# Output projection of a hybrid decoder layer: weights two tiles at a time, GpSimd's additions and low parts in pieces

## The chip, the cores and the metric

The kernel runs on one core of a Trainium2 chip. The metric is the device time of one execution in microseconds, lower is better; the time before is the median of three runs. A core has a matrix engine (TensorE, PE in the profile), a vector engine (VectorE, DVE), an activation engine (ScalarE, ACT), GpSimd (POOL) and SyncE (SP), which issues nearly all DMAs here. Each engine executes its own instructions strictly in the order in which they were put; engines wait for each other by semaphores.

## The reference

One inference step of one layer, for a prompt of 1024 positions and 8 samples of 8 new positions (N = 1088 columns in all):

```python
h = rms_norm(x, norm_mix_g)
proj = h @ w_in                       # a convolution branch and 12 attention heads
a = silu(layer_norm(depthwise_conv(a_val * sigmoid(a_gate))))
o = attend(q, k, v)                   # dilated windows, merged by their softmax denominators
x = x + concatenate([a, o]) @ w_out   # the output projection and the residual
h = rms_norm(x, norm_ffn_g)
x = x + (silu(conv3(h @ w_ffn_gate)) * (h @ w_ffn_up)) @ w_ffn_down
y = rms_norm(x, norm_final_g)
```

The change touches the fifth line: `w_out` is 1024 x 1024, `x` is 1024 features by 1088 columns, and the residual is the layer's input.

## The kernel before

Everything is kept transposed: 128 features on the partitions, positions along the row. A product in float32 is made of three matmuls on a faster 32-bit type: each operand is split into a high part (a copy that rounds, on ACT) and a low part (the difference, on DVE or GpSimd), and high·high, high·low and low·high are summed in PSUM.

The stages in order: the input projection (`project`), one pair of heads after the other; attention for the samples (`sample_attention`) and for the prompt (`prompt_heads`), which is written around the later projections; the output projection (`out_part` and, for the last part, `out_half`); the gated feed-forward part, as products of a Strassen-like scheme; the last projection and norm.

The input of the output projection is eight tiles of 128 features, `mixed[0]` to `mixed[7]`, spilled to DRAM as they are finished. It is done in three parts along the contraction, `PARTS = (3, 3, 2)` tiles. The first two parts are `out_part` with `k0 = 0` and `k0 = 3`, each over the eight output tiles m (L881). For each m, `load_w` (L155) loads 128 x 384 weights on SP's queue into a raw buffer `wr` (two buffers, tag WR), makes the high part `wh` on ACT (L163) and the low part `wl` on GpSimd (L165) (five buffers for both together, tag W), and `gemm` (L177) does three chunks of columns (384, 384, 320), or two halves of the columns up to HN = 544 where the rest is deferred. In the part with `k0 = 0` the sums are copied out of PSUM into `x2[m]` by ACT (L895) and DVE (L897). In the part with `k0 = 3` the residual `xr` is loaded (L888, three buffers, not before the last tile of the samples' cache was loaded), GpSimd adds it to `x2[m]` (L889), and DVE adds the sums (L893). The last three m of that part are kept back until the last head's weighted sums are issued (L899), as work for PE in that head's tail. The following stage takes its first weights and two tiles `eh`, `el` (L923) from the same buffers.

Attention for the prompt, per head and half of the positions: `load_head` loads queries and keys (L620, L628) and GpSimd reorders the queries (`qw`, L622); `scores` computes scores on PE (L675) into two PSUM banks `s`, and DVE takes them out with the running minimum (L679); `exchange` (L644) passes minima between classes by a small product (L653) and small DVE operations (L650, L656, L659); L704 and L705 take the minimum of two 128 x 4 tiles; ACT exponentiates (L716); PE transposes (L743) and takes the weighted sum (L764); at the end of a pair `normalise` divides (L774 to L783).

What order the instructions of one engine have is decided when the program is built: a planner simulates the program with costs of its own and puts on each engine the instruction that is ready, by priority, so that the matmuls of `out_part` fill the gaps between attention's steps. `tc.issue_after` and `high_priority` in the code constrain it. Buffers are handed on by the planner's waits: a tile's buffer comes free when the last reader of its earlier content is done.

Of the kernel before, what the change touches and what calls it, by code (L numbers as in the profile page):

```python
# [18 lines left out]
F32 = mybir.dt.float32  # L19
# [5 lines left out]
P = 128  # L25
D = 1024
# [4 lines left out]
N = S + NS  # L31
# [39 lines left out]
HN = N // 2  # L71
# [15 lines left out]
def trunk_kernel(tc, xT, w_in, w_first, w_out, w_gate, w_up, w_down, par, kc, vc, sa, sf, pmask, smask,  # L87
                 yT, kT, vT, ca, cas, cf):
    nc = tc.nc
    with (  # L90
# [8 lines left out]
        def nm(s):  # L99
            cnt[0] += 1  # L100
            return f"{s}_{cnt[0]}"
# [26 lines left out]
        def keep(s, w=N):  # L128
            return tp.tile([P, GW], F32, tag="T", name=nm(s))[:, :w]
# [22 lines left out]
            tc.add_manual_dep(later, earlier.name, mybir.DependencyInfo(mybir.DependencyClass.NoSync,  # L152
                                                                        mybir.DependencyReason.DATA))

        def load_w(src, nk, lo_eng, new=None):  # L155

            w = nk * P
            raw = wp.tile([P, w], F32, tag="WR", name=nm("wr"), bufs=WR)
            weights_read[0] = nc.sync.dma_start(raw if len(src.shape) == 2 else
                                                raw.rearrange("p (m c) -> p m c", m=src.shape[1]), src).ins  # L160
            new = new or [lambda s: wp.tile([P, w], F32R, tag="W", name=nm(s))] * 2
            hi = new[0]("wh")[:, :w]
            nc.scalar.activation(hi, raw, AF.Copy)  # L163
            lo = new[1]("wl")[:, :w]
            lo_eng.tensor_sub(lo, raw, hi.bitcast(F32))  # L165
            return hi.rearrange("p (k c) -> p k c", c=P), lo.rearrange("p (k c) -> p k c", c=P)

        cached = []
# [8 lines left out]
        def gemm(w, x, nk, evac, banks=None, chunks=CHUNKS):  # L177


            whi, wlo = w  # L180
            order = [(c, k) for c in range(len(chunks)) for k in range(nk)]
            if banks:
                order = [(c, k) for k in range(nk) for c in range(len(chunks))]
            ps = {}
            for c, k in order:
                t0, n = chunks[c]
                if k == 0:
                    ps[c] = bank(*(banks[c] if banks else gbank[0]))[:, :n]
                xh, xl = x[k]
                nc.tensor.matmul(ps[c], whi[:, k, :], xh[:, t0:t0 + n], start=(k == 0), stop=False)  # L190
                nc.tensor.matmul(ps[c], whi[:, k, :], xl[:, t0:t0 + n], start=False, stop=False)  # L191
                nc.tensor.matmul(ps[c], wlo[:, k, :], xh[:, t0:t0 + n], start=False, stop=(k == nk - 1))  # L192
                if k == nk - 1:
                    evac(ps[c], t0, n)
# [180 lines left out]
        def a_branch(i):  # L375
# [18 lines left out]
            if i == 0:  # L394
                first_gemms(sg, gp, se)
            else:
                gate = load_w(w_in[2 + i], KT, nc.vector)
                val = load_w(w_in[i], KT, nc.vector)
                gemm(gate, h, KT, ev_gate)
                gemm(val, h, KT, ev_val)  # L400
# [43 lines left out]

        def project(p, pump):
            W = [load_w(w_in[4 + 6 * c + p], KT, nc.gpsimd) for c in range(3)]
            dq = dp.tile([2, P, S], F32, name=nm("dq"))
            dk = dp.tile([2, P, S], F32, name=nm("dk"))
# [417 lines left out]
        x2 = []  # L866
        first = [0]

        def spare(s, w=N):
            return zt("R", "x2", KT - TB, s, GW)[:, :w]  # L870
# [7 lines left out]
        def out_part(k0, part):  # L878

            n = len(part)  # L880
            for m in range(KT):  # L881
                w = load_w(w_out[m, :, k0 * P:(k0 + n) * P], n, nc.gpsimd)
                if k0 == 0:
                    x2.append(keep("x2") if m >= KT - TB else spare("x2"))
                if k0 == PARTS[0]:
                    r = staged("xr")
                    with tc.issue_after(cached[8 * NS1 + X2]):
                        nc.sync.dma_start(r, xT[m * P:(m + 1) * P, :])  # L888
                    nc.gpsimd.tensor_add(x2[m], x2[m], r)  # L889

                def ev(ps, t0, n, x=x2[m]):
                    if k0:
                        nc.vector.tensor_add(x[:, t0:t0 + n], ps[:, :n], x[:, t0:t0 + n])  # L893
                    elif t0 in ONACT:
                        nc.scalar.activation(x[:, t0:t0 + n], ps[:, :n], AF.Copy)  # L895
                    else:
                        nc.vector.tensor_copy(x[:, t0:t0 + n], ps[:, :n])  # L897

                with tc.issue_after(weighed[0]) if k0 and m >= KT - BEHIND else nullcontext():  # L899
                    gemm(w, part, n, ev, chunks=CHUNKS if k0 == 0 or m not in ORDER[:DEFER] else HALF)  # L900

        def staged(s):
            return zt("G", "XR", XR, s)
# [12 lines left out]
        with tc.issue_after(turned_out[0]):  # L916
            nc.scalar.activation(sp.tile([P, 1], F32, name="table"), ones, AF.Sqrt)
        out_part(*part)
        for n in PARTS[1:-1]:
            out_part(*load_part(n, staged, g_part))  # L920
# [22 lines left out]
        def slot(tag, s, dt=F32R, w=HN):  # L943
            return zt("F", tag, 8, s, HN, dt)[:, :w]
# [53 lines left out]
        k0 = first[0]  # L998
        n = PARTS[-1]
# [36 lines left out]
        for h, tag in enumerate(("b11", "t2")):  # L1036
# [4 lines left out]
            for m0 in ORDER[h * 4:h * 4 + 4:2]:  # L1041
                raw = slot("b11", "wr", F32, 2 * n * P)
                queued(raw.rearrange("p (m c) -> p m c", m=2), w_out[m0:m0 + 2, :, k0 * P:].rearrange("m p c -> p m c"))
                hi, lo = early["b21"].pop() if early["b21"] else slot("b21", "wh", w=512), slot("b21" if m0 == ORDER[0] else "t3", "wl", w=512)
                with tc.issue_after(last_high):
                    last_high = parts_of(raw, hi, lo)
                hi, lo = [t.rearrange("p (k c) -> p k c", c=P) for t in (hi, lo)]
                for j in range(2):
                    wl[m0 + j] = hi[:, j * n:j * n + n], lo[:, j * n:j * n + n]
        for i in range(n1):  # L1050
            lo, hi = slot("b21", "ml"), slot("t3", "mh")
            raw = lo.bitcast(F32)
# [12 lines left out]
        for m in ORDER[:DEFER]:  # L1065
            hi, lo = [slot("b22", t, w=n1 * P) for t in ("wh", "wl")]
# [91 lines left out]
        raw = [slot("t2", "wr", F32, half) for _ in range(4)]  # L1158
# [362 lines left out]
        w, act = [], []  # L1521
# [140 lines left out]
        for i, (t0, n) in enumerate(TAIL):  # L1662
            r = []
# [20 lines left out]
        v, r, t = [sp.tile([P, 9], F32, tag=tag, name=nm(tag), bufs=2)[:, :nt] for tag in ("rv", "rr", "rt")]  # L1684
# [118 lines left out]
```

## Time and profile before

| | us |
|---|---|
| median of 3 runs | 1326.91 |
| lowest and highest | 1324.6, 1328.79 |
| profiled execution | 1329.6 |
| span of its instructions | 1327.8 |
| mean granted PE clock | 0.993 |
| output projection's residual additions (L889) | 500.2 to 529.5 of the span |

The profile is of one execution. Its page gives busy time by engine, the chain of work that ended last and the costliest groups of instructions; the trace behind it answers for any stretch of time, line or tile. Times within it are microseconds from the span's start; L889 is line 889 of the kernel. A DMA's issue is an instruction of SP's queue (SPq); its landing is later. The granted clock is the share of its full clock that PE was given.

### The profile page before, as it was taken

The page shows a single profiled execution, that of the slowest core. Times are in us where ns is not written, and L with a number is a line of the kernel's source. Part 1 is how long each engine was busy: PE and PEld are TensorE (multiplying, and loading weights), DVE is VectorE, ACT ScalarE, POOL GpSimd, SP SyncE. Part 2 cuts the span into 40 slices and gives each one's busy share as a digit, 9 for nine tenths or more (in the row PEclk, how much of TensorE's full clock was granted, in tenths as well). Part 3 has the DMA queues.
Part 4 walks back from the last instruction along what each step waited for, and adds up shares of the span by engine and source line. Part 5 has one row for each costly group of instructions (what it writes and reads, how often), then busy time and mean ns, then how long its engine had stood idle before and what let it go on. Part 6 is the DMA issues. An engine that isn't in the chain of part 4 may idle for free.

```text
span 1327.8 us, 26026 instructions
## 1 busy us (share of the span) xinstructions
PE 1294.9 (98%) x10336; PEld 1253.1 (94%) x10336; DVE 939.2 (71%) x1788; ACT 562.6 (42%) x1132; POOL 474.2 (36%) x389
## 2 busy tenths in 40 slices
PE   9999999999998998999999999999999999999997
PEld 9999898999977788899999999999999999999997
DVE  7479879555674657579976677676776659967656
ACT  7322221547584564565633323332333345334433
POOL 0121112111101016141656546565564544444611
PEclk9999999999999998999999999999999999999998
DMA  9248777564789996271023331232313395352403
GB/s 309 73 152 295 263 261 192 175 170 133 221 265 286 264 298 206 67 255 43 33 91 123 107 108 63 93 123 91 122 42 114 104 342 206 108 178 96 157 32 104
DMA packets 93658, 211.43 MB, mean 159 GB/s; under 512 B 13920, under 2 KB 42720, under 8 KB 93536
## 3 DMA queue, kind: packets, MB, share of 16 engines
q1 hardware_dynamic: 92672, 208.76, 47.9%
q8 instruction: 81, 1.33, 0.4%
q10 hardware_dynamic: 864, 1.01, 0.2%
q14 instruction: 41, 0.34, 0.1%
HBM read 153.69 MB, written 56.04 MB: 158 GB/s over the span
## 4 chain that ended last, share of the span: by engine, by line
PE 78%; DVE 11%; DMA 7%; ACT 2%; issue 1%; SPq 0%; DVEq 0%; ACTq 0%
PE g L190 6%; PE g L191 6%; PE g L192 6%; PE py L955 4%; PE py L958 4%; PE py L957 4%; PE g L955 4%; PE g L958 4%; PE g L957 4%; PE pz L955 3%; PE pz L958 3%; PE pz L957 3%; PE px L955 3%; PE px L958 3%; PE px L957 3%; PE s L675 3%
## 5 line engine op out<-in xcount | busy, mean ns | idle before, releaser
L165 POOL TENSOR_TENSOR wl<-wr,wh 128x1024 fp32r<-128x1024 f32 (+1 forms) x34 | 62.0, 1823 | 313.9 <-PE g L192 191.1
L190 PE MATMUL g<-xh,wh 128*128 128x384 f32 (+1 forms) x472 | 156.8, 332 | 0.9 <-DVE qkv L467 0.9
L192 PE MATMUL g<-xh,wl 128*128 128x384 f32 (+1 forms) x472 | 155.3, 329 | 0.0
L191 PE MATMUL g<-xl,wh 128*128 128x384 f32 (+1 forms) x472 | 155.2, 329 | 0.0
L955 PE MATMUL g<-ux,as 128*128 128x272 f32 x504 | 145.1, 288 | 0.6 <-DVE x L1595 0.6
L958 PE MATMUL g<-ux,as 128*128 128x272 f32 x504 | 145.3, 288 | 0.0
L957 PE MATMUL g<-ux,as 128*128 128x272 f32 x504 | 144.7, 287 | 0.0
L1109 POOL TENSOR_TENSOR wb<-wr,wb 128x512 fp32r<-128x512 f32 x79 | 116.3, 1484 | 50.1 <-ACT wb L1108 50.1
L1505 POOL TENSOR_TENSOR as<-ar,as 128x640 fp32r<-128x640 f32 (+1 forms) x56 | 89.1, 1602 | 104.6 <-ACT as L1504 92.1
L1108 ACT ACTIVATE wb<-wr 128x512 fp32r<-128x512 f32 x79 | 49.7, 629 | 163.2 <-DVE wr L1143 104.3
L955 PEld LDWEIGHTS g<-ux,as 128*128 128x128 f32 x504 | 95.0, 189 | 1.0 <-issue 1.0
L1109 POOL TENSOR_TENSOR wa<-wr,wa 128x512 fp32r<-128x512 f32 x40 | 62.4, 1561 | 90.9 <-ACT wa L1108 89.0
L958 PEld LDWEIGHTS g<-ux,as 128*128 128x128 f32 x504 | 94.8, 188 | 0.0
L957 PEld LDWEIGHTS g<-ux,as 128*128 128x128 f32 x504 | 94.6, 188 | 0.0
L716 ACT ACTIVATE y<-y,m 128x128 f32<-128x128 f32 (+1 forms) x192 | 88.5, 465 | 10.6 <-DVE m L704 9.3
L1373 DVE SCALAR_TENSOR_TENSOR fc<-gb,prm,fc 128x1104 f32<-128x1104 f32 x44 | 82.2, 1888 | 14.7 <-ACT fc L1371 14.4
L190 PEld LDWEIGHTS g<-xh,wh 128*128 128x128 f32 x472 | 88.7, 188 | 3.0 <-DVE qkv L467 1.5
L191 PEld LDWEIGHTS g<-xl,wh 128*128 128x128 f32 x472 | 88.8, 188 | 0.1
L192 PEld LDWEIGHTS g<-xh,wl 128*128 128x128 f32 x472 | 88.8, 188 | 0.0
L417 DVE SCALAR_TENSOR_TENSOR cacc<-gp,prm,cacc 128x1024 f32<-128x1024 f32 x60 | 84.2, 1404 | 0.1
L679 DVE CUSTOM_DVE_ANT_0 y<-s,pmk 128x128 f32<-128x128 f32 (+1 forms) x192 | 63.6, 375 | 25.5 <-PE s L675 22.7
L163 ACT ACTIVATE wh<-wr 128x1024 fp32r<-128x1024 f32 (+1 forms) x36 | 29.6, 821 | 121.0 <-PE g L192 93.4
(413 smaller groups left out, 4309.3 us busy)
## 6 DMA issues: line engine op xcount, KB each, us to landing
cr<-in_kc SPq DMA_DIRECT2D x24, 768.0 KB, 8.5
cr<-in_vc SPq DMA_DIRECT2D x24, 768.0 KB, 8.7
ux<-ub SPq DMA_DIRECT2D x63, 272.0 KB, 4.2
kk<-dk SPq DMA_DIRECT2D x48, 256.0 KB, 6.3
wr<-in_w_in SPq DMA_DIRECT2D x20, 512.0 KB, 5.2
wr<-in_w_gate SPq DMA_DIRECT2D x20, 512.0 KB, 3.3
wr<-in_w_up SPq DMA_DIRECT2D x20, 512.0 KB, 4.6
ub<-u SPq DMA_DIRECT2D x18, 544.0 KB, 4.0
```

What stands on the lines that cost most here:

```text
L190: nc.tensor.matmul(ps[c], whi[:, k, :], xh[:, t0:t0 + n], start=(k == 0), stop=False)
L191: nc.tensor.matmul(ps[c], whi[:, k, :], xl[:, t0:t0 + n], start=False, stop=False)
L192: nc.tensor.matmul(ps[c], wlo[:, k, :], xh[:, t0:t0 + n], start=False, stop=(k == nk - 1))
L417: eng.scalar_tensor_tensor(acc[:, :S], gp[:, j:j + S], col(w0 + j), acc[:, :S], op0=ALU.mult, op1=ALU.add)
L679: nc.vector.tensor_tensor_reduce(out=y[:, o:o + n], in0=ps[:, o:o + n], in1=mask, op0=ALU.add, op1=ALU.min, scale=1.0, scalar=3e38, accum_ ...
L716: nc.scalar.activation(y, y, AF.Exp, bias=m[:, 4 * g + i:4 * g + i + 1], scale=-1.0, accum_out=den[:, g, 2 * hd + u, i:i + 1])
L955: nc.tensor.matmul(ps, whi[:, k, :], xh[:, t], start=(start and k == 0), stop=False, skip_group_check=True)
L957: nc.tensor.matmul(ps, whi[:, k, :], xl[:, t], start=False, stop=False, skip_group_check=True)
L958: last = nc.tensor.matmul(ps, wlo[:, k, :], xh[:, t], start=False, stop=(stop and k == nk - 1), skip_group_check=True).ins
L1109: nc.gpsimd.tensor_sub(lo, x, hi.bitcast(F32))
L1373: nc.vector.scalar_tensor_tensor(c[:, :W], gb[i][:, t:t + W], col(C_FW + 3 * f + t), c[:, :W], op0=ALU.mult, op1=ALU.add)
L1505: nc.gpsimd.tensor_sub(lo, raw, hi.bitcast(F32))
```

## The change

`load_w` gets a parameter `cut`: the low part is made by instructions of at most `cut` columns instead of one. `out_part` calls it for every second m, with the weights of m and m + 1 in one DMA and one raw buffer (128 x 768), one high part of 768 columns on ACT, and three low parts of 256 columns on GpSimd; each m takes its half of both. The residual is added in four pieces of 272 columns. The bytes, the matmuls and the DVE instructions stay the same.

```diff
-        def load_w(src, nk, lo_eng, new=None):
+        def load_w(src, nk, lo_eng, new=None, cut=D):
...
             lo = new[1]("wl")[:, :w]
-            lo_eng.tensor_sub(lo, raw, hi.bitcast(F32))
+            for c in range(0, w, cut):
+                t = slice(c, min(c + cut, w))
+                lo_eng.tensor_sub(lo[:, t], raw[:, t], hi.bitcast(F32)[:, t])
...
             for m in range(KT):
-                w = load_w(w_out[m, :, k0 * P:(k0 + n) * P], n, nc.gpsimd)
+                if m % 2 == 0:
+                    both = load_w(w_out[m:m + 2, :, k0 * P:(k0 + n) * P].rearrange("m p c -> p m c"), 2 * n, nc.gpsimd,
+                                  cut=2 * P)
+                w = [t[:, m % 2 * n:m % 2 * n + n] for t in both]
...
-                    nc.gpsimd.tensor_add(x2[m], x2[m], r)
+                    for c in range(0, N, HN // 2):
+                        t = slice(c, c + HN // 2)
+                        nc.gpsimd.tensor_add(x2[m][:, t], x2[m][:, t], r[:, t])
```

`load_w` is also called for `w_in` in the input projection, with `cut` at its default of 1024 columns, which is one instruction as before.

## The prediction

> **What bounds the kernel now.** The page of the profile is read first: busy time by engine and the chain that ended last.
>
> ```profile
> PE 1294.9 (98%) x10336; PEld 1253.1 (94%) x10336; DVE 939.2 (71%) x1788; ACT 562.6 (42%) x1132; POOL 474.2 (36%) x389
> ...
> PE 78%; DVE 11%; DMA 7%; ACT 2%; issue 1%; SPq 0%; DVEq 0%; ACTq 0%
> ```
>
> TensorE (PE) is busy for all but 1327.8 − 1294.9 = 32.9 us of the span, so an edit that touches no matmul can win only time in which PE stands idle or runs at a lower granted clock. The second view is therefore busy time by stretches of 10 us over the output projection, which runs interleaved with the last attention heads. Columns: stretch, its length, busy us of PE, PEld, DVE, ACT and POOL with their instructions, granted clock, DMA share, GB/s.
>
> ```profile
> 500.00:510.00 10.00, 6.17 (x34) 5.85 (x33) 9.39 (x25) 4.92 (x19) 9.78 (x4) 0.71 0.86 257
> 510.00:520.00 10.00, 10.00 (x122) 9.35 (x122) 8.29 (x20) 3.45 (x11) 7.19 (x5) 0.95 0.61 154
> ```
>
> One stretch stands out: from 500 to 510 PE has 6.17 us of work, the clock falls to 0.71, and GpSimd (POOL) is busy for 9.78. The same view cut at the stall, and the waits of PE from 410 to 560 (who waited, for whom, us in total, times, longest):
>
> ```profile
> 502.30:506.06 3.76, 0.00 (x1) 0.01 (x1) 3.69 (x8) 2.98 (x13) 3.76 (x3) 0.76 0.68 218
> 506.06:511.00 4.94, 4.94 (x20) 4.94 (x21) 3.86 (x18) 0.38 (x1) 4.52 (x3) 0.50 1.03 291
> ```
>
> ```profile
> PE s L675 <- DVE st L679: 3.8, 1, 3.8
> PE o L764 <- DMA vw<-dv: 2.6, 1, 2.6
> PE ss L568 <- DMA cr<-in_kc: 2.6, 1, 2.6
> ```
>
> PE stands still for 3.76 us and then works 4.94 us at half clock. It waits for the minimum of the scores (L679, on VectorE, DVE), which frees the score banks. What held L679 is in the order of time on DVE and POOL (start, us, engine, line):
>
> ```profile
> 500.24 2.50 DVE L705 TENSOR_TENSOR m<-st,xr 128x4 f32<-128x4 f32 x1
> 502.67 0.27 DVE L659 TENSOR_REDUCE xr<-xf 128x32 f32<-128x128 f32 x1
> 502.97 2.22 DVE L774 TENSOR_TENSOR dn<-xr,den 128x16 f32<-128x16 f32 x1
> 505.23 0.42 DVE L679 CUSTOM_DVE_ANT_0 y<-s,pmk 128x256 f32<-128x256 f32 x1
> ...
> 505.57 0.42 DVE L679 CUSTOM_DVE_ANT_0 y<-s,pmk 128x256 f32<-128x256 f32 x1
> 505.92 0.08 DVE L679 DVE_READ_ACCUMULATOR2_ANT st<- 128x1 f32 x1
> ```
>
> ```profile
> 500.22 9.87 POOL L889 TENSOR_TENSOR x<-x,xr 128x1088 f32<-128x1088 f32 x4 [5.35 <-DMA xr<-in_xT]
> ```
>
> ```profile
> L705 DVE TENSOR_TENSOR m<-st,xr x24: 146/152/2503, 237.6 to 544.1; 128x4 f32<-128x4 f32 x24
> ```
>
> L705 works on 4 columns. Its median is 152 ns (the row has minimum, median, maximum); here it took 2.50 us, and ended when the first of POOL's four residual additions did (500.22 + 9.87/4 = 502.69). L774 met the second one and ended with it. So a small DVE operation on SBUF that meets a POOL addition waits for that whole instruction, here twice in a row: this, not the amount of POOL's work, makes PE's stall. Between two additions DVE does get in (L705 ended before L774 was held again). L679, which reads PSUM, took its usual 0.42 beside the third addition.
>
> **The change, part by part.** The sum is made against the profiled execution, 1329.6 us (span 1327.8 and 1.8 around it).
>
> *The residual additions in pieces.* Eight instructions of 1088 columns become 32 of 272; two of 384 columns for the low parts become three of 256. POOL has rows for nearly these sizes:
>
> ```profile
> L889 POOL TENSOR_TENSOR x<-x,xr 128x1088 f32<-128x1088 f32 x8 | 20.1, 2528 | 11.2 <-DMA xr<-in_xT 11.2
> L165 POOL TENSOR_TENSOR wl<-wr,wh 128x384 fp32r<-128x384 f32 x16 | 16.2, 1012 | 119.9 <-PE g L192 73.2 <-PE r L192 16.4 <-PE ss L558 15.0
> L1652 POOL TENSOR_TENSOR x<-x,rb 128x256 f32<-128x256 f32 x4 | 2.9, 740 | 20.9 <-ACT rb L241 20.9
> ```
>
> 256 columns cost 740 ns; the slope from 384 to 1088 columns is (2528 − 1012)/704 = 2.15 ns a column, so 272 cost 0.740 + 16 × 0.00215 = 0.775 us. Replay the stall: the first piece runs 500.22 to 501.00; L705 ends at 501.15; L659 adds 0.27 (501.42); L774 meets the second piece, which began near 501.15 and ends at 501.93, and ends at 502.11; two L679 with their accumulator reads take 505.23 to 506.00, 0.77 us, so the bank is free at 502.9. PE's previous matmul ended here:
>
> ```profile
> 501.89 0.34 PE L192 MATMUL g<-mh,wl 128*128 128x384 f32 x1
> 506.06 2.08 PE L675 MATMUL s<-kk,qw 128*128 128x256 f32 x8 [3.83 <-DVE st L679]
> ```
>
> The gap shrinks from 3.83 to 502.9 − 502.23 = 0.7 us: **−3.1 us**. Bounds: 0, if DVE is not let in between pieces; −3.83, if L705 and L774 meet none.
>
> *The half clock behind it.* 4.94 us at 0.50 are 2.47 us of work at full clock, so without the drop **−2.5 us**; bounds 0 and −2.5. Whether a gap brings a drop isn't read from its length alone:
>
> ```profile
> 410.00:413.00 3.00, 1.10 (x8) 0.81 (x6) 0.00 (x0) 0.49 (x1) 0.00 (x0) 1.00 1.02 313
> 413.00:416.40 3.40, 2.65 (x25) 2.32 (x26) 0.49 (x3) 0.00 (x0) 0.00 (x0) 1.00 1.04 416
> ...
> 547.00:549.50 2.50, 1.36 (x6) 0.90 (x8) 0.34 (x2) 2.15 (x8) 0.00 (x0) 0.83 0.91 278
> 549.50:552.50 3.00, 3.00 (x18) 2.25 (x17) 0.90 (x4) 0.05 (x1) 0.00 (x0) 0.58 0.47 160
> 552.50:555.00 2.50, 1.53 (x12) 1.06 (x10) 1.81 (x3) 1.73 (x4) 0.00 (x0) 1.00 0.00 0
> ```
>
> A gap of 2.65 us (the wait for vw) left the clock at 1.00, while 1.14 us of idle time in 2.5 us was followed by 0.58. I take the whole drop as gone, since a gap of 0.7 among busy matmuls is the smallest of these. [...]
>
> *POOL's longer work.* The additions grow from 20.1 to 32 × 0.775 = 24.8 us, the low parts from 16.2 to 24 × 0.740 = 17.8 us. POOL's idle time covers that: from 500 to 520 it is busy 9.78 + 7.19 of 20 us. What is queued behind on POOL is the reordering of a head's queries (qw, L622):
>
> ```profile
> 511.46 1.04 POOL L622 CAST qw<-qs 128x1024 fp32r<-128x1024 f32 x1
> ```
>
> ```profile
> 516.66 1.09 PE L675 MATMUL s<-kk,qs 128*128 128x128 f32 x8
> ...
> 521.34 0.83 PE L675 MATMUL s<-kk,qw 128*128 128x128 f32 x5
> ```
>
> Four additions take 16 × 0.775 = 12.4 instead of 9.87 us, and a pair's low part 2.2 instead of 1.0, so L622 would start 3.7 us later and end near 516.2. PE, 5.6 us earlier, would want it at 521.34 − 5.6 = 515.7: **+0.5 us**, or nothing if the planner puts the cast between pieces. SyncE (SP) is held by the same additions, for the three buffers of xr:
>
> ```profile
> 496.04 7.04 SPq L888 DMA_DIRECT2D xr<-in_xT  x4
> 503.17 1.09 SPq L620 DMA_DIRECT2D qs<-dq  x2
> ```
>
> and for that L620:
>
> ```profile
> DMA to landing us min/median/max: 5.0/5.4/5.9
> ```
>
> The fourth xr waits for the first addition (4 × 0.775 = 3.1 instead of 2.5 us), so the queries behind it leave 0.6 us later. They take 5.4 us to land (503.8 + 0.5 + 5.4 = 509.7 for the second) and are wanted at 516.66 − 5.6 = 511.1: nothing.
>
> *Two tiles at once.* Sixteen loads of 192 KB become eight of 384 KB, the same bytes. The five buffers of high and low parts and the two raw buffers then hold 4.5 tiles (0.88 MB) more ahead, moved in front of attention's loads in the one SP queue: at the 291 GB/s above 3.0 us, the upper end, since PE already waits for DMAs twice (2.6 and 2.6). But those early loads are issued where the queue is not full:
>
> ```profile
> 360.00:370.00 10.00, 10.00 (x75) 9.37 (x74) 4.08 (x17) 3.35 (x10) 0.00 (x0) 1.00 0.19 78
> 370.00:380.00 10.00, 9.48 (x90) 8.73 (x88) 7.64 (x40) 7.42 (x25) 2.50 (x4) 1.00 0.80 214
> ```
>
> Free shares of 0.81 and 0.20 of 10 us are 10 us of transfer, three times what is needed. I take **+0.5 us**, near the lower end. ACT's splits (16 of 384 columns become 8 of 768) get no dearer and lie off the path: nothing. The gain that deeper filling may bring lies in the tail above, 547 to 555: idle 1.14 + 0.97 and clock losses of 0.17 × 1.36 + 0.42 × 3.00 = 1.5, in all 3.6 us. I count none of it, since those gaps are waits inside the last head, not for weights.
>
> **Sum:** −3.1 − 2.5 + 0.5 + 0.5 = **−4.6 us**: 1325.0 for a profiled execution. The median before, 1326.9, lies 2.7 us under the profiled one; the same sum on it gives **1322.3 us**.
>
> **Rivals.**
>
> 1. *The clock drop was the profiled execution's own.* For it: the 2.7 us between the profile and the median are nearly the 2.5 of the drop. Against it: drops follow smaller gaps too, as shown. The gain is then 3.1 − 1.0 = 2.1: 1324.8. [...]
>
> 2. *The stall survives or moves*, the change not doing what it says: POOL's pieces follow each other so closely that DVE loses each time, or the planner, which orders every engine by its own estimates, puts other DVE operations of the path beside the adds. Against it: DVE got in between the additions above. Price: nothing gained, 1.0 paid, 1327.9.
>
> 3. *SP's queue is blocked longer: slower.* SP issues in order, and a weight load waits there until the raw buffer's low part is done, which waits for matmuls:
>
> ```profile
> SPq L159 <- POOL wl L165: 25.2, 5, 9.5
> ```
>
> The longest such wait is 9.5 us; a pair is released by two tiles instead of one, so a wait of 19 us is possible. A head's queries are used 516.66 − 503.17 = 13.5 us after their issue; from there on it costs. PE would stop 5.5 us and, as at 506, lose 2.5 more: 8.0, less the 4.6 gained, is +3.4: 1330.3. Twice, it is 1338. Against it: buffers for five tiles need fewer loads late in the stage.
>
> **How the numbers follow.** Forecast 50% (its own range 1318 to 1324.5, reaching down by the 0.7 left of the gap and the 3.6 of the tail), rival 1 15%, rival 2 17%, rival 3 18%. A measurement of this kernel tells about 0.3%, 4.0 us, from no change: faster means below 1322.9, slower above 1330.9. Faster: 0.8 of the forecast and a fifth of rival 1, 0.43. Slower: 0.15 of rival 3 and 0.02 of rival 2, 0.17. Within: 0.40. The range 1318 to 1331 leaves out the lowest of the forecast (some 5%) and most of rival 3 (some 15%).
>
> **What would show it.** In the profile after: L889 32 times near 0.78 us; L705 and L774 nowhere above about 0.95 us; PE's longest wait for L679 below 1 us; clock 1.00 where the residual additions run; POOL's busy time up by 6 us; w_out loads of 384 KB, with SP's wait for L165 no longer than 9.5 us. Wrong would make it: a PE wait of more than 3 us for qs, qw, kk or vw, or a new one for DVE elsewhere from 380 to 570; weight loads standing on the chain; or a time that moves in stages that the diff doesn't touch, where the planner has reordered work.

## The result, and the profile after

| | before | after |
|---|---|---|
| median of 5 runs each, same chip (us) | 1325.54 | 1320.51 |
| lowest and highest | 1324.6, 1328.79 | 1316.28, 1322.68 |
| profiled execution, its span | 1329.6, 1327.8 | 1317.16, 1315.4 |
| mean granted PE clock | 0.993 | 0.997 |

The ratio of the times is 0.9949, with the interval [0.9925, 0.9974]: 5.0 us faster by the medians, where 4.6 were predicted. The two profiled executions differ by 12.4 us, more than the medians do. So the change is judged by the medians, and the profiles are used for where time is lost.

The page after: busy time by engine, and the chain that ended last.

```profile
PE 1290.3 (98%) x10336; PEld 1250.4 (95%) x10336; DVE 926.6 (70%) x1788; ACT 561.1 (43%) x1124; POOL 479.9 (36%) x421
...
PE 81%; DVE 11%; DMA 5%; issue 1%; ACT 1%; SPq 0%; POOL 0%; DVEq 0%; ACTq 0%
```

PE still bounds the kernel. POOL is busy for 5.7 us more (479.9 against 474.2); the residual's pieces had been priced at 4.7 us more and the low parts' at 1.6. The stretch with the stall, by 10 us, after:

```profile
500.00:510.00 10.00, 9.86 (x129) 8.96 (x128) 8.74 (x28) 5.80 (x20) 7.50 (x10) 1.00 0.98 265
510.00:520.00 10.00, 10.00 (x74) 9.39 (x74) 5.85 (x17) 2.64 (x4) 6.98 (x11) 1.00 0.83 273
```

PE is busy for 9.86 of the first 10 us instead of 6.17, and the clock is 1.00 instead of 0.71 and 0.95. What PE waited for between 380 and 570, after (lines stand two, later seven higher than before: L679 is L681, L889 is L896):

```profile
PE o L766 <- DMA vw<-dv: 2.7, 1, 2.7
...
PE s L677 <- DVE st L681: 0.4, 1, 0.4
```

The wait of 3.83 us is down to 0.4. The wait for vw stays as it was (2.6). POOL in order of time after, and the minimum, median and maximum of the residual pieces:

```profile
514.66 8.78 POOL L896 TENSOR_TENSOR x<-x,xr 128x272 f32<-128x272 f32 x12 [3.02 <-DMA xr<-in_xT]
523.40 2.13 POOL L167 TENSOR_TENSOR wl<-wr,wh 128x256 fp32r<-128x256 f32 x3
525.48 5.86 POOL L896 TENSOR_TENSOR x<-x,xr 128x272 f32<-128x272 f32 x8
```

```profile
L896 POOL TENSOR_TENSOR x<-x,xr x32: 750/774/960, 502.5 to 530.5; 128x272 f32<-128x272 f32 x32
```

A piece takes 774 ns at the median (775 were worked out). From 514.66 to 531.34 POOL runs 23 of them without a break: such an unbroken row of POOL instructions is called a train below. Of the small DVE operations that meet this train, the one held longest, after:

```profile
520.47 0.80 DVE L707 TENSOR_TENSOR m<-st,xr 128x4 f32<-128x4 f32 x1
```

It waited for one piece. Each of these signs is as the prediction named it. Two things are not yet answered by it: whether the pieces bring the gain, or the weights in pairs do, which came with them; and whether the clock would have dropped in most runs before.

The part of the stage ahead of the residual additions gives a first hint. Busy time from 400 to 500 and from 500 to 560, before, after, and in a kernel that has the pieces alone (resid_only below), in this order:

```profile
400.00:500.00 100.00, 93.55 (x916) 81.52 (x916) 57.12 (x229) 52.89 (x153) 11.44 (x13) 1.00 0.96 284
500.00:560.00 60.00, 52.93 (x480) 48.17 (x479) 38.15 (x111) 29.42 (x91) 26.00 (x14) 0.91 0.46 136
```

```profile
400.00:500.00 100.00, 97.06 (x997) 85.48 (x995) 59.15 (x252) 57.36 (x170) 14.39 (x19) 1.00 0.95 286
500.00:560.00 60.00, 57.59 (x500) 54.27 (x499) 36.16 (x101) 29.08 (x80) 37.45 (x47) 1.00 0.54 165
```

```profile
400.00:500.00 100.00, 98.53 (x950) 86.02 (x949) 61.48 (x248) 56.01 (x164) 14.97 (x18) 1.00 0.99 293
500.00:560.00 60.00, 56.73 (x524) 52.19 (x525) 35.64 (x106) 30.91 (x91) 34.35 (x42) 0.97 0.49 144
```

Between 400 and 500 the profiled execution before left PE idle for 6.5 us, after for 2.9. But resid_only, which has the weight loads of before, left only 1.5: the waits for DMAs there differ between executions of nearly the same order, so that difference of 3.5 us need not be the change's. From 500 on, after and resid_only both gain on before, after by 4.7 us of PE and with a clock of 1.00 against 0.91.

### The profile page after: what moved, and what is told of

Same layout as the page of the kernel before. It is cut to its first block, busy times and chain, and to the rows that moved or that the text cites. A ratio compares the mean times of both kernels' runs of the same rounds, so it can differ in the third digit from the quotient of the medians.

```text
span 1315.4 us, 26030 instructions
## 1 busy us (share of the span) xinstructions
PE 1290.3 (98%) x10336; PEld 1250.4 (95%) x10336; DVE 926.6 (70%) x1788; ACT 561.1 (43%) x1124; POOL 479.9 (36%) x421
## 4 chain that ended last, share of the span: by engine, by line
PE 81%; DVE 11%; DMA 5%; issue 1%; ACT 1%; SPq 0%; POOL 0%; DVEq 0%; ACTq 0%
PE g L192 6%; PE g L194 6%; PE g L193 6%; PE g L965 5%; PE g L964 5%; PE g L962 5%; PE py L962 5%; PE py L964 5%; PE py L965 5%; PE pz L964 3%; PE pz L965 3%; PE pz L962 3%; PE o L766 3%; PE px L962 3%; PE px L965 3%; PE s L677 3%
## 5 line engine op out<-in xcount | busy, mean ns | idle before, releaser
L167 POOL TENSOR_TENSOR wl<-wr,wh 128x256 fp32r<-128x256 f32 (+1 forms) x42 | 61.7, 1485 | 263.3 <-PE g L194 116.2
L681 DVE CUSTOM_DVE_ANT_0 y<-s,pmk 128x128 f32<-128x128 f32 (+1 forms) x192 | 63.6, 376 | 28.3 <-PE s L677 25.8
L1602 DVE TENSOR_TENSOR x<-g,x 128x544 f32<-128x544 f32 x76 | 52.5, 715 | 35.7 <-PE g L965 35.7
```

What stands on the lines that cost most here:

```text
L681: nc.vector.tensor_tensor_reduce(out=y[:, o:o + n], in0=ps[:, o:o + n], in1=mask, op0=ALU.add, op1=ALU.min, scale=1.0, scalar=3e38, accum_ ...
```

## The experiments

The theories, as the expectations name them:

- **A**: a small DVE operation is held by the POOL instruction that it meets, so the length of POOL's pieces sets the wait, and the residual in pieces brings the gain.
- **B**: the weights in pairs bring it, by what they do to the order: **B1** because more tiles' weights are ready ahead, **B2** because the planner's new order happens to put other work beside the held operations.
- **C**: the half clock was the profiled execution's own, so that less is gained.
- **S** (formed after the first four runs): a train of short pieces can keep a DVE operation out for many pieces, while pieces of 544 and more let it in at the next end.

All ratios are to the kernel before on the same chip, with 95% intervals; 12 runs of each kernel, 29 or 35 of before.

| weights and low parts | residual 1088 | 544 | 272 | 136 |
|---|---|---|---|---|
| single tiles, low part 384 | 1 (before) | 0.9970 [0.9949, 0.9990] | 0.9979 [0.9964, 0.9994] | |
| single, high and low in one buffer | 0.9996 [0.9978, 1.0014] | 0.9968 [0.9947, 0.9988] | | |
| pairs, low part 768 whole | 0.9996 [0.9978, 1.0013] | 0.9984 [0.9966, 1.0002] | 1.0000 [0.9980, 1.0020] | |
| pairs, low parts of 256 | 0.9953 [0.9930, 0.9976] | 0.9950 [0.9925, 0.9975] | 0.9953 [0.9930, 0.9976] (after, again) | 1.0023 [1.0006, 1.0040] |

### The pieces alone: resid_only

To the kernel before, only the residual in pieces of 272.

```diff
-                    nc.gpsimd.tensor_add(x2[m], x2[m], r)
+                    [nc.gpsimd.tensor_add(x2[m][:, c:c + HN // 2], x2[m][:, c:c + HN // 2], r[:, c:c + HN // 2])
+                     for c in range(0, N, HN // 2)]
```

> Only the residual in four pieces of 272 columns; weights one tile at a time as before, low parts whole. The planned order of PE differs from before in 46 of 8862 lines only. Theory A (a small DVE operation is held for a whole GpSimd instruction, and the piece's length sets the wait): the 3.83 us wait of PE for L679 falls below 1 us, the half clock behind it goes, 3 to 6 us faster than before. Theory B (the pairs and the order that the planner makes of them bring the gain): within 1.5 us of before. Theory C (the clock drop was one execution's own): 2 to 3 us faster, the wait gone in the trace.

Measured: 1322.33 us, 0.9979 [0.9964, 0.9994], about 2.8 us. The small operations that were held before (L705 2.50, L774 2.22), here with minimum, median and maximum:

```profile
L705 DVE TENSOR_TENSOR m<-st,xr x24: 145/155/803, 238.1 to 534.0; 128x4 f32<-128x4 f32 x24
```

```profile
L774 DVE TENSOR_TENSOR dn<-xr,den x6: 180/182/628, 286.4 to 540.2; 128x16 f32<-128x16 f32 x6
```

The pieces do what A says of the wait: it falls to one piece, and time is gained, in an order of instructions that is nearly that of before. The size of the gain doesn't tell A from C: 2.8 us lies where C expected it (2 to 3) and just below A's 3 to 6, and the interval, 0.8 to 4.8 us, covers much of both.

### The change without the pieces: pairs_cut

To the kernel after, the residual whole again; pairs and low parts of 256 stay.

```diff
-                    for c in range(0, N, HN // 2):
-                        t = slice(c, c + HN // 2)
-                        nc.gpsimd.tensor_add(x2[m][:, t], x2[m][:, t], r[:, t])
+                    nc.gpsimd.tensor_add(x2[m], x2[m], r)
```

> The changed kernel with the residual added whole (1088 columns); pairs and cut low parts stay. PE, DVE and ACT have the changed kernel's order, line for line. Theory A: one or two small DVE operations near the first additions take over 2 us again, PE waits 2 us or more for L681, time 3 to 6 us above the changed kernel. Theory B: the changed kernel's time within 1.5 us. Theory C: 2 to 3 us above the changed kernel.

Measured: 1318.70 us, 0.9953 [0.993, 0.9976]: all of the change's gain, without the pieces. B had expected the time of after within 1.5 us, A 3 to 6 us more. PE, DVE and ACT have exactly the order of after. POOL, DVE and PE of this kernel in order of time:

```profile
503.78 2.51 POOL L894 TENSOR_TENSOR x<-x,xr 128x1088 f32<-128x1088 f32 x1 [2.98 <-DMA xr<-in_xT]
```

```profile
504.57 1.76 DVE L652 TENSOR_TENSOR xe<-st,pmk 128x16 f32<-128x16 f32 x1
```

```profile
504.44 0.86 PE L596 MATMUL ss<-cr,spt 128*32 128x128 f32 x24
...
505.34 0.84 PE L596 MATMUL ss<-cr,spt 128*32 128x128 f32 x24
506.73 0.55 PE L783 MATMUL t<-ident,db 128*128 128x128 f32 x3 [0.54 <-DVE db L780]
```

DVE is held here too, 1.76 us until the end of the addition that it met, and 1.87 us by another one at 516.34. But PE has the samples' products (L596) to do meanwhile, until 506.18, and stands still for 0.54 us instead of 3.76. In the order of after the held operation has cover on PE; in that of before it had none. So against this stall the pieces are one remedy and the order another, and the two do not add up. Whether the cover is all that the order brings is asked again with pairs_only below.

### Other lengths in the order of after: resid_544, resid_136

To the kernel after, pieces of 544 (shown); resid_136 has `HN // 4` in place of `HN`, pieces of 136.

```diff
-                    for c in range(0, N, HN // 2):
-                        t = slice(c, c + HN // 2)
+                    for c in range(0, N, HN):
+                        t = slice(c, c + HN)
```

> The changed kernel with the residual in two pieces of 544 columns, same order of PE, DVE and ACT. Theory A: a held DVE operation takes up to 1.36 us (0.185 + 544 x 0.00215), PE's wait for L681 up to about 1.5 us, time 0 to 2.5 us above the changed kernel. Theory B and C: the changed kernel's time within 1.5 us.

> The changed kernel with the residual in eight pieces of 136 columns, same order of PE, DVE and ACT. Theory A: a held DVE operation takes at most 0.48 us more than its own time, GpSimd's additions grow from 24.8 to about 31 us, time within 1.5 us of the changed kernel, or later by the queries' reordering behind the additions. Theory B: the same within 1.5 us.

Measured: 1318.60 us for 544, not told apart from 272 or 1088; and 1330.52 us for 136, 1.0023 [1.0006, 1.004], some 10 us slower than 272, with the same order on PE, DVE and ACT. No theory had expected that. resid_136 on POOL, DVE and PE in order of time, and by 10 us:

```profile
518.60 9.15 POOL L896 TENSOR_TENSOR x<-x,xr 128x136 f32<-128x136 f32 x21 [1.67 <-DMA xr<-in_xT]
527.69 2.12 POOL L167 TENSOR_TENSOR wl<-wr,wh 128x256 fp32r<-128x256 f32 x3
529.75 8.18 POOL L896 TENSOR_TENSOR x<-x,xr 128x136 f32<-128x136 f32 x19
```

```profile
525.78 12.18 DVE L652 TENSOR_TENSOR xe<-st,pmk 128x16 f32<-128x16 f32 x1
```

```profile
538.48 0.69 PE L192 MATMUL g<-mh,wh 128*128 128x384 f32 x1 [9.69 <-DVE x L900]
```

```profile
530.00:540.00 10.00, 1.52 (x5) 1.52 (x6) 10.00 (x10) 0.00 (x0) 7.93 (x19) 0.63 0.40 111
```

L652 works on 16 columns, 0.175 us at its median. Here it took 12.18 us, and ended at 537.96, when the train did (529.75 + 8.18 = 537.93): some 23 pieces and the three low parts of POOL ended in that time without its being let in. PE waited 9.69 us for the sums queued behind it on DVE (L900), and the clock dropped (0.63 from 530 to 540, 0.86 from 540 to 550). Hence theory S.

### The pairs without the cut: pairs_only, no_cut

Both are the kernel after with the low part of a pair in one instruction of 768; pairs_only has the residual whole too.

```diff
                     both = load_w(w_out[m:m + 2, :, k0 * P:(k0 + n) * P].rearrange("m p c -> p m c"), 2 * n, nc.gpsimd,
-                                  cut=2 * P)
+                                  )
```

> Only the pairs: one load, one high part and one low part of 768 columns for two tiles; residual whole. Its planned order of PE differs from before and from the changed kernel. Theory A (piece length) is left with the case that it has nothing to win here: no gain, or a loss where a low part of 1.84 us holds DVE. Theory B1 (weights for five tiles instead of two and a half stand ready, so that PE's order has matmuls between the steps of attention): 5 to 8 us faster than before, PE's waits for kc and L681 gone. Theory B2 (the planner's order differs, and its luck decides): anything from 8 us faster to 3 slower.

> The changed kernel with the low parts of a pair in one instruction of 768 columns; residual in pieces of 272. PE, DVE and ACT have the order of the pairs alone. Against the pairs alone it shows the residual's pieces in that order. Theory A: 2 us or more faster than the pairs alone. Theory B1 and B2: within 1.5 us of the pairs alone.

Measured: 1325.35 us (0.9996) and 1327.07 us (1.0000): neither gains, and no_cut misses the 2 us or more against pairs_only that A expected. Against pairs_cut, pairs_only differs in the cut of the low parts alone, and 0.9996 stands against 0.9953 [0.993, 0.9976]. The cut also changes the planner's order, so these two runs don't separate its length from its order.

Where pairs_only loses is not at the additions. Its small operations are held there as well (the longest 2.57 us, L706 at 525.91), and PE has other work meanwhile. Busy time from 400 to 500 and from 500 to 560, of pairs_only and then of pairs_cut:

```profile
400.00:500.00 100.00, 94.04 (x904) 83.78 (x903) 54.58 (x240) 55.26 (x177) 9.99 (x9) 0.97 0.91 269
500.00:560.00 60.00, 57.55 (x537) 53.45 (x536) 45.83 (x112) 31.47 (x82) 29.16 (x15) 1.00 0.52 155
```

```profile
400.00:500.00 100.00, 97.10 (x998) 85.72 (x996) 58.79 (x255) 56.29 (x168) 13.53 (x19) 1.00 0.93 281
500.00:560.00 60.00, 57.12 (x490) 53.46 (x491) 39.88 (x100) 29.91 (x80) 32.71 (x22) 1.00 0.52 161
```

From 500 on the two are alike. Ahead of it PE waited 3.0 us for cached values (L596) and 2.8 us for keys (L677) in pairs_only, and the clock from 400 to 500 was 0.97 instead of 1.00; in pairs_cut no wait there was longer than 1.7 us. Such waits of one execution prove little, but the granted clocks of all runs point the same way: what a run lost to the clock, estimated as its span times the share of the clock that was not granted, averages 9.0 us over the 24 runs of pairs_only and no_cut_544 (below), whose profiles have no stall at the additions, and 5.9 us over the 36 of pairs_cut, resid_544 and after_again, which have the order of after. So cover at the additions does not make the gain by itself, and what the cut brings against pairs_only lies ahead of them, at least in part.

With the pieces of 272, no_cut shows S a second time (POOL, DVE, PE in order of time, then by 10 us):

```profile
518.05 14.57 POOL L895 TENSOR_TENSOR x<-x,xr 128x272 f32<-128x272 f32 x20 [5.32 <-DMA xr<-in_xT]
532.53 1.85 POOL L167 TENSOR_TENSOR wl<-wr,wh 128x768 fp32r<-128x768 f32 x1
534.29 2.95 POOL L895 TENSOR_TENSOR x<-x,xr 128x272 f32<-128x272 f32 x4
```

```profile
528.91 8.37 DVE L652 TENSOR_TENSOR xe<-st,pmk 128x16 f32<-128x16 f32 x1
```

```profile
537.33 0.64 PE L655 MATMUL s<-xe,pmk 128*128 128x32 f32 x2 [5.66 <-DVE xe L652]
```

```profile
530.00:540.00 10.00, 4.34 (x36) 4.10 (x33) 9.34 (x8) 1.24 (x3) 7.24 (x9) 0.75 0.45 141
```

Again L652 came out with the train's last instruction (534.29 + 2.95 = 537.24, L652 ends at 537.28), here with pieces of 272, the very length of the change.

### Five tiles ahead without pairs: packed

For B1: to the kernel before, the high and the low part of a tile share one of the five buffers, so that five tiles are ready ahead, by single loads. The residual is whole.

```diff
-                w = load_w(w_out[m, :, k0 * P:(k0 + n) * P], n, nc.gpsimd)
+                t = wp.tile([P, D], F32R, tag="W", name=nm("whl"))
+                w = load_w(w_out[m, :, k0 * P:(k0 + n) * P], n, nc.gpsimd,
+                           [lambda s: t[:, :n * P], lambda s: t[:, n * P:2 * n * P]])
```

> The kernel before with one edit: high and low part of a tile's weights (384 columns each) lie in one buffer of 1024 columns, so that five tiles' weights can stand ready without pairs; loads of 192 KB, whole residual and whole low parts as before. Theory B1: 5 to 8 us faster than before, as the pairs. Theory B2: anything, no nearer to the pairs than to before. Theory A: no gain, one DVE operation over 2 us near the first residual additions with PE waiting behind it.

Measured: 1325.33 us, 0.9996 [0.9978, 1.0014]. Depth alone gains nothing; and where shorter pieces take the stall out of this kernel as out of before (packed_544 and before_544 below), it gains nothing either (0.9968 and 0.9970). So B1 falls. The run shows more: the stall of before comes back in another order, with other lines. POOL, DVE, PE in order of time, and by 2 us:

```profile
503.59 5.33 POOL L891 TENSOR_TENSOR x<-x,xr 128x1088 f32<-128x1088 f32 x2 [0.62 <-DMA xr<-in_xT]
```

```profile
504.48 2.02 DVE L704 TENSOR_TENSOR m<-st,xr 128x4 f32<-128x4 f32 x1
...
507.45 1.51 DVE L650 TENSOR_TENSOR xe<-st,pmk 128x16 f32<-128x16 f32 x1
```

```profile
509.35 0.66 PE L781 MATMUL t<-ident,db 128*128 128x128 f32 x4 [3.36 <-DVE db L778]
```

```profile
510.00:512.00 2.00, 2.00 (x13) 2.00 (x12) 1.93 (x7) 1.59 (x6) 0.00 (x0) 0.71 1.21 169
512.00:514.00 2.00, 2.00 (x8) 1.91 (x8) 1.23 (x2) 0.00 (x0) 1.62 (x1) 0.50 0.78 176
```

Two small operations are held by two whole additions one after the other, PE stands still for 3.36 us, and then works at half clock (0.50 from 512 to 514): the picture of before.

### Pieces of 544 in three orders: before_544, packed_544, no_cut_544

The residual in two halves, put into before, packed and no_cut. packed_544 and no_cut_544 keep the order of PE and DVE of the kernels that they come from; before_544 differs from resid_only in a few lines on PE.

```diff
+                    for c in range(0, N, HN):
+                        nc.gpsimd.tensor_add(x2[m][:, c:c + HN], x2[m][:, c:c + HN], r[:, c:c + HN])
```

> The kernel before with the residual in two pieces of 544 alone. PE's order differs from that with 272 alone in 10 lines. Theory A and S: L705 and L774 at most 1.5 us each, PE's wait for L679 under 2 us, 2 to 5 us faster than before (1321 to 1324), about as with 272. Theory B2: within 1.5 us of before.

> High and low part in one buffer, loads of one tile, and the residual in two pieces of 544; PE, DVE and ACT have the order of the packed kernel. Theory A and S: what held DVE there for 2.0 to 2.6 us falls to 1.5 or less and PE's wait of 3.4 us for db to under 1, 2 to 5 us faster than packed (1320 to 1323). Theory B2: within 1.5 us of packed, 1325.

> Pairs with the low parts whole and the residual in two pieces of 544 instead of four of 272: every engine but GpSimd has the order of that kernel with 272, line for line. Theory S (a train of short pieces can keep one DVE operation out for many pieces, as L652 for 8.37 us there, and pieces of 544 or more let it in at the next end): no DVE operation held over 1.5 us, PE's wait of 5.7 us for L652 gone, 3 to 7 us faster than with 272 (1320 to 1324). Theory B2 (the planned order decides, the piece's length doesn't): within 1.5 us of it and of the pairs alone.

Measured: before_544 0.9970 [0.9949, 0.9990]; packed_544 0.9968 [0.9947, 0.9988] against packed's 0.9996, PE's wait for L778 down to 1.1 us; no_cut_544 1323.90 us, 0.9984 [0.9966, 1.0002], against no_cut's 1.0000: the medians differ by 3.2 us, the intervals overlap, and the waits for DMAs differ too. In no_cut_544 the small operation held longest by the additions (1.40 us, at 522.51, on 4 columns) waited for one piece, not a train:

```profile
L707 DVE TENSOR_TENSOR m<-st,xr x24: 146/155/1397, 238.5 to 533.5; 128x4 f32<-128x4 f32 x24
```

### The held operations by themselves: micro

A kernel that computes nothing of the reference and writes zeros. POOL adds 5 x 1088 columns in pieces of 1088, 544, 272 or 136, the last two also with a small memset between pieces. DVE meanwhile alternates operations with a PSUM input, of changing length (L135), and small products of two SBUF tiles of 16 columns (L136). Each is done three times.

```python
for _ in range(ROUNDS):                        # 5
    for c in range(0, N, width):
        nc.gpsimd.tensor_add(x[:, c:c + width], x[:, c:c + width], xr[:, c:c + width])
        if spaced: nc.gpsimd.memset(gap, 0.0)
for i, w in enumerate(WIDTHS):                 # 12
    nc.vector.tensor_add(filled[:, :w], bank[:, :w], st[:, :1].to_broadcast([P, w]))
    nc.vector.tensor_mul(small[i % 2], st, own)
```

> Nothing of the reference is computed; the outputs are zeros. GpSimd adds 5 x 1088 columns in one train, in pieces of 1088, 544, 272, 136, and of 272 and 136 with a memset between the pieces, three times each; beside it DVE does 12 multiplications of 128x16 with both inputs in SBUF, each after an addition that reads PSUM. If DVE is let in at the end of any piece: the longest small multiplication is a piece and its own 0.17 us, about 2.7, 1.4, 0.95, 0.65 us, with or without memsets. If pieces that follow each other closely keep it out: single ones last for many pieces, up to the rest of a train (12 to 19 us), most of all at 136, and the memset ends that.

Measured: alone L136 takes 0.16 to 0.17 us; the longest that was let in at the next end took 2.44, 1.31, 0.66 and 0.44 us beside pieces of 1088, 544, 272 and 136, so A's sizes hold. But three operations in each repeat took longer (POOL and DVE in order of time; the bracket is the time for which DVE had waited before):

```profile
6.86 12.72 POOL L131 TENSOR_TENSOR xs<-xs,xr 128x1088 f32<-128x1088 f32 x5 [6.42 <-DMA xr<-in_xT]
23.15 12.90 POOL L131 TENSOR_TENSOR xs<-xs,xr 128x544 f32<-128x544 f32 x10 [3.57 <-ACT xs L126]
38.42 14.32 POOL L131 TENSOR_TENSOR xs<-xs,xr 128x272 f32<-128x272 f32 x20 [2.37 <-ACT xs L126]
53.97 17.15 POOL L131 TENSOR_TENSOR xs<-xs,xr 128x136 f32<-128x136 f32 x40 [1.22 <-ACT xs L126]
```

```profile
51.11 1.67 DVE L136 TENSOR_TENSOR small<-st,own 128x16 f32<-128x16 f32 x1 [5.28 <-ACT done L138]
...
68.62 2.52 DVE L136 TENSOR_TENSOR small<-st,own 128x16 f32<-128x16 f32 x1 [8.95 <-ACT done L138]
...
104.47 2.79 DVE L136 TENSOR_TENSOR small<-st,own 128x16 f32<-128x16 f32 x1 [11.20 <-ACT done L138]
```

The first came into the train of 272 and ended with it (38.42 + 14.32 = 52.74; 52.78), the second into that of 136 (71.12; 71.14), each past more than one end of a piece. The third came into 136 with memsets between, where the memset was expected to end it: it did not. With 272 and memsets the same operation took 0.28 us. The three repeats agree to 0.01 us, in the phase of the two engines too, so each case is one sample. All three held ones followed a stand of DVE; why that train of 272 with memsets let its operation in is open.

### The change once more: after_again

> The changed kernel once more, for a median of as many runs as the experiments have: 1318.5 to 1322 us. A DVE operation held for many pieces (over 3 us) may stand in its slower runs; if the profile falls on one, near the trains of additions.

Measured: 1320.19 us over 12 runs (1314.56 to 1327.71), 0.9953 [0.993, 0.9976]. It agrees with the first 0.9949. The profile (of a run of 1320.64 us) has no operation held for many pieces: the longest beside a train of additions took 0.83 us. resid_544 and pairs_cut lie 1.6 and 1.5 us below by their medians, less than their intervals tell: no kernel tried beats the change.

## Why the prediction was right in its size, and what in it was wrong

**The stall (−3.1).** The mechanism holds: in two orders, before's and packed's, small DVE operations held by two additions in a row stop PE for 3.8 and 3.4 us, and shorter pieces gain 0.21 to 0.30% there, 2.8 to 4.0 us (resid_only, before_544, and packed_544 against packed with 0.28%). That is the whole of their gain, the clock and POOL's longer work included, for which the prediction's terms give 5.1 (3.1 + 2.5 − 0.5). The replay's sizes hold as well (0.80 and 0.63 us for L705 and L774 in resid_only; PE's wait 0.4 after, 0.7 predicted).

**What failed is where the gain was booked.** The prediction gave all of it to the pieces, and of the pairs it said "I count none of it" and "+0.5 us". In the kernel after it is the pairs with their cut low parts that carry the gain: pairs_cut, without the pieces, is at 0.9953, and adding pieces of 544 or 272 changes nothing. At the stall its trace shows how: the planner's order puts the samples' products beside the held operation. That is not all of it, since pairs_only has such cover and gains nothing; what else the cut brings stays open. That the stall "survives or moves" by reordering was seen as a risk (rival 2), not as a gain. That the sum came out so near is partly luck: the clock term was too large, the two costs of 0.5 were not seen, and a gain of the pairs was left out.

**The half clock (−2.5).** In the profile after it went with the gap: 1.00. PE's gaps of 3.36 (packed), 5.66 (no_cut) and 9.69 us (resid_136) each came with a drop too (the clock was 0.50 from 512 to 514 in packed, and 0.75 and 0.63 from 530 to 540 in the other two), so drops do belong to gaps. But not to each, and not in each execution: after and after_again are the same kernel, PE waits for vw in both, 2.74 us until 414.66 and 2.59 us until 416.10, and only the second wait brought a drop (after, then after_again):

```profile
416.00:418.00 2.00, 2.00 (x18) 1.83 (x17) 1.18 (x4) 1.19 (x2) 0.00 (x0) 1.00 1.05 425
```

```profile
416.10 0.40 PE L766 MATMUL o<-ph,vw 128*64 128x256 f32 x1 [2.59 <-DMA vw<-dv]
```

```profile
418.00:420.00 2.00, 2.00 (x11) 1.84 (x10) 0.64 (x3) 1.19 (x2) 0.00 (x0) 0.50 1.04 423
```

The size of the term can be estimated from all runs, again as the span times the share of the clock that was not granted. The profiled execution before lost 9.3 us so, the 99 runs of that kernel 7.3 on average: rival 1 was right that some of the loss was that execution's own. resid_only and before_544 lost 6.3 over 24 runs, the 70 runs of before on their two chips 7.5. So the pieces save about 1 us of clock in an average run, with an uncertainty as large as that, and not 2.5. Only the clock over a whole run is known, not how often the drop came at this stall.

**POOL's longer work (+0.5).** POOL's busy time grew as priced, but nothing waited: after, the last reordering of queries starts at 498.0, ahead of all residual additions.

```profile
L624 POOL CAST qw<-qs x12: 1037/1040/1399, 214.5 to 498.0; 128x1024 fp32r<-128x1024 f32 x12
```

The planner had moved it, and the prediction had named such a move as the case of no cost.

**The DMAs (+0.5) and rival 3.** PE's longest wait for a DMA is 2.7 us after, 2.6 before, and SP's longest wait for a low part between 380 and 570 fell:

```profile
SPq L159 <- POOL wl L167: 3.3, 2, 2.1
```

2.1 us instead of 9.5. A pair released by two tiles did not block the queue; rival 3 did not occur.

**Rival 2's mechanism is real, elsewhere.** "POOL's pieces follow each other so closely that DVE loses each time" was held against by one observation with pieces of 1088. It happened with 136 (12.18 us) and, in the order of no_cut, with 272 (8.37 us). In the kernel after, a train of 23 pieces of 272 met only operations that were let in, the longest after 0.80 us. What made the difference was not shown, and nothing in the change as made protects it from such a hold.

**Open.** Whether the cut of the low parts to 256 works by its length or by the order that the planner makes of it, and what it brings ahead of the additions; how often the half clock came at the stall; and what decides whether a train lets a waiting operation in.

## What to carry to other kernels

A small DVE operation can wait for the GpSimd instruction that it meets (2.50 us beside 1088 columns here), and here that mattered only where the matmul engine had nothing else in its order at that moment (it stood for 3.76 us in before, for 0.54 us in pairs_cut): look there first, since other work beside it can hide the wait as shorter pieces cut it. Don't cut further than is needed: pieces of 544 gained in both orders whose stall they were put against, and were never seen to keep DVE out for longer than one piece (1.40 us at most), while unbroken trains of 272 and 136 did (8.37 and 12.18 us). Where a planner makes the order, run each part of a change by itself, because an edit that "only" moves loads can carry the whole gain. And don't take a loss to the clock from one profile: the same wait brought a drop in one execution and none in another (2.59 us and a clock of 0.50, 2.74 us and 1.00).

## What the runs showed of the hardware that was not expected

A waiting DVE operation was not always let in at the next end of a GpSimd instruction. In five cases beside unbroken trains of short ones it was kept out until the train's end, past more than one end of a piece: 12.18 us (136 columns, 0.474 us each at the median), 8.37 us (272, 0.774 us each in the kernel after), and 1.67, 2.52 and 2.79 us in the kernel made for it. Beside pieces of 544 and 1088 the longest wait in any run was one piece (1.40 us in no_cut_544; 2.57 us in packed and in pairs_only).

Shorter pieces also cost GpSimd itself: the same 5440 columns took 12.72, 12.90, 14.32 and 17.15 us in pieces of 1088, 544, 272 and 136 in micro.
